# A hybrid decoder layer on one Trainium2 core: the second half's output projection by token tiles, its weights split further ahead, and the FFN operands made in two rounds

## The chip, the core and the metric

The kernel runs on one core of a Trainium2 chip. The core has a matrix engine (TensorE, PE in the profile; PEld is its weight load), a vector engine (VectorE, DVE), a scalar engine (ScalarE, ACT), GpSimd (POOL) and a queue engine for transfers (SyncE, SP). Each engine carries out its own instructions in the order in which they stand; engines wait for each other through semaphores. The metric is the device time in microseconds (us) of one execution; shorter is better. Before the change it is 1290.92 us, the median of three runs (1289.92 to 1294.27).

## What is computed

One decoder layer for a prompt of 1024 tokens and 8 single-token samples, width 1024, everything in float32. What matters here is the middle: a mixer (attention and retention) gives `mix`, an output projection follows, then a layer norm, then a SwiGLU FFN with 2816 hidden columns and a second layer norm.

```python
y = jnp.concatenate([att, ret], -1) @ w_out                       # mixer's end: 1024 x 1024
yp = layer_norm(DEEPNORM_ALPHA * yp + (1.0 + gtp) * mp, ln1_w, ln1_b)
shp, scp, gtp = ada_mod(c_prompt, w_ada_ffn, b_ada_ffn)
g, u = jnp.split((yp * (1.0 + scp) + shp) @ w_up, 2, axis=-1)
fp = (silu(g) * u) @ w_down
yp = layer_norm(DEEPNORM_ALPHA * yp + (1.0 + gtp) * fp, ln2_w, ln2_b)
```

## The kernel before

**Arithmetic.** A float32 product is made of three matmuls of rounded operands (`mm3`, L213 to L217): each operand is split into a high half (a cast by ScalarE) and a low half (a subtraction by VectorE that waits for that cast), and high x high, high x low and low x high are summed in a PSUM bank. There are 8 banks of 128 x 512. All larger tiles in SBUF come from one pool of 46 pages of 128 x 1040 (L186); a new tile waits for the last readers of the page that it takes.

**Order.** `Merge` (L103 to L175) runs one main generator (matmuls) and weaves side generators between its steps by estimated costs; a side generator can wait for a name in the set `done`. A scheduler then fixes each engine's order from the priorities in which this code was run.

**Output projection** (`out_proj`, L1108 to L1166). The tokens are two halves of 512, each of four tiles of 128. A half is done in two column groups of 512 (`cg`), a group in four weight units `kp` of 256 rows. The units of the second half are numbers 54 to 57 (first column group) and 58 to 61 (second); `raw57`, `wh57`, `wl57` are unit 57 as loaded, its high half and its low half. For each unit the four tiles take their products in turn, so all four banks `pout0` to `pout3` of a group are complete only at its end. Sample rows take the unsplit weights in eight small matmuls per group (`poutz`). Then each tile is evacuated: VectorE multiplies the bank by the gate (`otmp`, L1157) and adds the scaled residual (`xr`, L1158).

`depth = [2, 1, 0]` (L285) says how many units ahead of the current one are loaded, get their high half and get their low half (`w_get`, L287). `w_mid` asks for the next unit's low half in the middle of a unit.

**Layer norm 1** (`ln1_tile`, L1202). For each token tile, once both column groups of its half are out (`("out", half)`): statistics on VectorE (L1176, L1181), a power on GpSimd (L1183), normalisation on ScalarE (L1197). `ln1_s` does the same for the sample rows and transposes them (`h2ps`, L1223).

**FFN operands** (`h2_group`, L1235). Group `g` is the half `g`. It needs all four normalised tiles of its half. For each of four blocks `j` it transposes eight 128 x 128 pieces on TensorE (`h2p`), applies the modulation on ScalarE (`ht`, L1253), splits two quarters (`hb`, L1258/L1259), forms four sums and differences (`ts`, L1263 to L1265), splits these (`hs`, L1301/L1302) and splits a last quarter (`hc`, L1271/L1272). A block does all of this before the next one begins.

**FFN up** (`up`, L1489). The product is done by a seven-product scheme with the steps 1, 2, 6, 7, 5, 3, 4 (L1296). Steps 1 and 2 use `hb`, step 3 uses `hc`, the others use `hs`. There are 22 weight matrices. Matrix 0 is first applied to group 0 and then to group 1 (L1583 to L1586); from matrix 1 on both groups are taken together. Each matrix is loaded in two pieces `wr` (L1311), VectorE forms four sums `sb`, `sa` (L1320 to L1323), and four splits `wa`, `wb`, `wc`, `wd` follow. `up_prep` (L1352) sets out these steps by a list of due times; matrix 1 and later wait for the name `ahead`. Matrix 0's load and sums are written down inside `out_proj` at `kp` 2 and 3 of the last column group.

The stages follow each other by these lines (L1764 to L1768): `out_proj(0, False)`; layer norm and operands of half 0 beside `out_proj(1, True)`; layer norm and operands of half 1 beside `ffn()`.

Of the kernel before, what the change touches and what calls it, by code (L numbers as in the profile page):

```python
# [177 lines left out]
def emit(ctx, tc, I, O):  # L178
# [928 lines left out]

    def out_proj(half, with_s):  # L1108
        yield ("need", ("att", half))
        for cg in range(2):  # L1110
            ps = [bank(f"pout{t}") for t in range(4)]
            psz = None
            prev = None
            for kp in range(4):
# [25 lines left out]
                if with_s and kp % 2 == 1:  # L1140
# [4 lines left out]
                    for q in range(4):  # L1145
                        w = (prev if q < 2 else raw)[:, (q % 2) * 512:(q % 2) * 512 + 512]
                        PE.matmul(psz[32 * q:32 * q + 32, :], lhsT=mixTs[:, 4 * (kp // 2) + q, :], rhs=w,
                                  start=kp == 1, stop=kp == 3)
# [4 lines left out]
            cs = slice(cg * 512, (cg + 1) * 512)
            for t in range(4):
                x = xr[half * 4 + t]
                tmp = tmp512("otmp")
                V.tensor_tensor(out=tmp, in0=ps[t], in1=gates[1][:, cs], op=ALU.mult)  # L1157
                V.scalar_tensor_tensor(out=x[:, cs], in0=x[:, cs], scalar=ALPHA, in1=tmp, op0=ALU.mult, op1=ALU.add)  # L1158
            if with_s:
                tmp = tmp512("otmp")  # L1160
                samp_sum(tmp[0:8], psz, 512)
                V.tensor_tensor(out=tmp[0:8], in0=tmp[0:8], in1=gates[1, "s"][0:8, cs], op=ALU.mult)
                x = xrs[0]
                V.scalar_tensor_tensor(out=x[0:8, cs], in0=x[0:8, cs], scalar=ALPHA, in1=tmp[0:8], op0=ALU.mult,
                                       op1=ALU.add)
# [36 lines left out]
    def ln1_tile(t):  # L1202
        yield "need", ("out", t // 4)
# [31 lines left out]
    def h2_group(g):  # L1235
# [8 lines left out]
        for j in range(4):  # L1244
            ht = page(f"ht{g}_{j}")
            hv = ht[:, 0:4 * n].rearrange("p (s b c) -> p s b c", s=2, b=2)
            h3 = ht[:, 0:4 * n].rearrange("p (q c) -> p q c", q=4)
            for s in range(2):
# [12 lines left out]
            HB[g, j] = hb  # L1261
            ts = page(f"ts{g}_{j}")
# [8 lines left out]
            A.copy(out=hc[:, o:o + n], in_=h3[:, 3])  # L1271
            V.tensor_sub(out=hc[:, o + n:o + 2 * n], in0=h3[:, 3], in1=f(hc[:, o:o + n]))  # L1272
# [543 lines left out]
```

## Time and profile before

| what | value |
| --- | --- |
| median of three runs | 1290.92 us |
| the profiled execution, its own time | 1291.37 us |
| its span, first to last instruction | 1289.5 us |
| mean granted TensorE clock | 0.971 |
| before the output projections | 0 to 423.5 us |
| both halves' output projections | 423.5 to 576.3 us |
| first up products until TensorE runs without gaps | 576.3 to 625 us |
| up products (last one starts near 1055 us), then down products (from 1059.8 us) | to the end |

In rows of the timeline the columns are: start in us from the span's start, duration in us, engine, line, operation, tile written <- tiles read, sizes, and how many instructions were merged. A bracket gives the idle time just before the row and what ended it. In a table of windows each engine's busy time in a stretch stands in front of its number of instructions; the last three columns are granted clock (1.00 is full speed), share of the transfer engines, and GB/s.

### The profile page before, as it was taken

The numbers are of one execution on the slowest core, as the hardware profiler recorded it, in microseconds if no ns is written. First come the engines' busy times: TensorE is split into PE (matmuls) and PEld (weight loads), VectorE is DVE, ScalarE is ACT, GpSimd is POOL, SyncE is SP. The second block draws the span as 40 slices with busy tenths as digits, with TensorE's granted clock in tenths as the row PEclk, the third lists the DMA queues.
The fourth block names the chain that finished last, engine by engine and source line by source line (L and its number), as shares of the span: only waits on it lengthen the run. The fifth ranks groups of instructions, "written<-read, shape, count | busy, mean of one in ns | idle before, by whom it ended". The sixth has DMA issues, their size and how long they took to land.

```text
span 1289.5 us, 20190 instructions
## 1 busy us (share of the span) xinstructions
PE 1222.2 (95%) x7922; PEld 1031.0 (80%) x7922; DVE 883.6 (69%) x1712; ACT 449.2 (35%) x812; POOL 159.0 (12%) x170
## 2 busy tenths in 40 slices
PE   8999979899999989696999999999999998999996
PEld 5877756688777667475899999999999986888885
DVE  2456675786654586767676776676676759849697
ACT  2335523344552223516232232323232234524420
POOL 0000032321002242002011110111011110000021
PEclk8999989999999989887999999999999999999998
DMA  9732477152226431602254444444354389846631
GB/s 285 234 110 66 138 250 250 49 176 78 64 67 211 146 101 35 204 1 99 76 178 156 131 138 142 156 148 163 107 179 157 123 313 392 290 158 206 205 129 66
DMA packets 144135, 199.07 MB, mean 154 GB/s; under 512 B 8139, under 2 KB 85171, under 8 KB 144024
## 3 DMA queue, kind: packets, MB, share of 16 engines
q1 hardware_dynamic: 133512, 161.37, 39.1%
q0 software_dynamic: 10528, 36.42, 7.4%
q8 instruction: 62, 1.02, 0.3%
q14 instruction: 33, 0.27, 0.1%
HBM read 155.02 MB, written 43.77 MB: 154 GB/s over the span
## 4 chain that ended last, share of the span: by engine, by line
PE 37%; issue 34%; DVE 8%; POOL 5%; DMA 2%; ACT 1%; POOLq 0%; DVEq 0%; SPq 0%; ACTq 0%
PE dn L216 4%; PE dn L215 4%; PE dn L217 4%; PE pin L215 4%; PE pin L217 3%; PE pin L216 3%; PE pout L216 2%; PE pout L217 2%; PE pout L215 2%; POOL fd L1440 1%; POOL fs L1444 1%; PE adab L874 1%; POOL ws L1473 1%; DVE z L1550 1%; DMA z<-yd 1%
## 5 line engine op out<-in xcount | busy, mean ns | idle before, releaser
L215 PE MATMUL pin<-wh,hT 128*128 128x512 f32 (+1 forms) x320 | 129.3, 408 | 0.1
L216 PE MATMUL pin<-wl,hT 128*128 128x512 f32 (+1 forms) x320 | 125.2, 391 | 3.8 <-DVE wl L281 3.8
L217 PE MATMUL pin<-wh,hT 128*128 128x512 f32 (+1 forms) x320 | 125.2, 392 | 0.4 <-DVE hT L340 0.4
L215 PE MATMUL up<-hb,wa_h 128*128 128x256 f32 (+1 forms) x352 | 100.5, 286 | 0.5 <-ACT tp L1388 0.5
L216 PE MATMUL up<-hb,wa_h 128*128 128x256 f32 (+1 forms) x352 | 100.4, 285 | 0.0
L217 PE MATMUL up<-hb,wa_l 128*128 128x256 f32 (+1 forms) x352 | 100.0, 285 | 0.0
L215 PEld LDWEIGHTS pin<-wh,hT 128*128 128x128 f32 x320 | 61.0, 191 | 26.9 <-issue 13.8
L281 DVE TENSOR_TENSOR wl<-raw,wh 128x1024 fp32r<-128x1024 f32 (+1 forms) x62 | 73.4, 1187 | 7.3 <-ACT wh L269 3.6
L217 PEld LDWEIGHTS pin<-wh,hT 128*128 128x128 f32 x320 | 61.6, 193 | 15.6 <-DVE hT L340 1.7
L216 PEld LDWEIGHTS pin<-wl,hT 128*128 128x128 f32 x320 | 61.8, 193 | 14.5 <-DVE wl L281 4.3
L215 PEld LDWEIGHTS up<-hb,wa_h 128*128 128x128 f32 x352 | 67.3, 191 | 2.1 <-ACT tp L1388 1.0
L1407 ACT ACTIVATE sg<-sg 128x256 f32<-128x256 f32 (+1 forms) x66 | 27.5, 419 | 118.5 <-DVE sg L1406 118.5
L216 PEld LDWEIGHTS up<-hb,wa_h 128*128 128x128 f32 x352 | 67.2, 191 | 0.5 <-DVE hb L1259 0.3
L217 PEld LDWEIGHTS up<-hb,wa_l 128*128 128x128 f32 x352 | 67.2, 191 | 0.1
L216 PE MATMUL pout<-wl,mh 128*128 128x512 f32 x128 | 54.8, 428 | 12.9 <-DVE wl L281 12.9
L269 ACT CAST wh<-raw 128x1024 fp32r<-128x1024 f32 (+1 forms) x62 | 62.6, 1022 | 11.4 <-DMA raw<-in_w_in 6.7
L1183 POOL TENSOR_TENSOR lrs<-lrs,cst 128x1 f32<-128x1 f32 (+1 forms) x18 | 23.7, 1320 | 284.0 <-DVE lrs L1182 218.9
L215 PE MATMUL pout<-wh,mh 128*128 128x512 f32 x128 | 53.2, 424 | 4.2 <-ACT wh L269 4.2
L1412 DVE TENSOR_TENSOR uc<-up,tp 128x256 f32<-128x256 f32 x66 | 28.2, 427 | 39.4 <-PE up L217 39.3
L1406 DVE TENSOR_TENSOR sg<-up,tp 128x256 f32<-128x256 f32 (+1 forms) x66 | 27.8, 423 | 38.4 <-PE up L217 38.4
L1440 POOL DMA_DIRECT2D fd<-sg x33 | 19.8, 600 | 278.7 <-DVE sg L1413 278.7
L217 PE MATMUL pout<-wh,ml 128*128 128x512 f32 x128 | 53.8, 420 | 0.0
(502 smaller groups left out, 3687.8 us busy)
## 6 DMA issues: line engine op xcount, KB each, us to landing
wr<-in_w_up SPq DMA_DIRECT2D x44, 512.0 KB, 5.3
raw<-in_w_in SPq DMA_DIRECT2D x38, 512.0 KB, 3.9
adr<-in_w_ada_ffn SPq DMA_DIRECT2D x24, 512.0 KB, 4.1
wd<-in_w_down SPq DMA_DIRECT2D x22, 512.0 KB, 5.1
dr<-fs SPq DMA_DIRECT2D x44, 256.0 KB, 2.9
dr<-ws SPq DMA_DIRECT2D x44, 256.0 KB, 3.3
fd<-sg POOLq DMA_DIRECT2D x33, 256.0 KB, 3.9
dr<-fd SPq DMA_DIRECT2D x33, 256.0 KB, 7.3
```

Source lines behind the costliest of these rows:

```text
L215: PE.matmul(ps, lhsT=ah, rhs=bh, start=start, stop=False, skip_group_check=onto)
L216: PE.matmul(ps, lhsT=ah, rhs=bl, start=False, stop=False, skip_group_check=onto)
L217: PE.matmul(ps, lhsT=al, rhs=bh, start=False, stop=stop, skip_group_check=onto)
L269: A.copy(out=h[:, 0:n], in_=src[:, 0:n])
L281: V.tensor_sub(out=l[:, 0:n], in0=src[:, 0:n], in1=f(h[:, 0:n]))
L874: PE.matmul(b[32 * q:32 * q + 32, :], lhsT=cT[:, k2 * 4 + q, :], rhs=rr[q // 2][:, (q % 2) * 512:(q % 2) * 512 + 512], start=k2 == 0, stop ...
L1183: G.tensor_tensor(out=rs[0:rows, 0:1], in0=rs[0:rows, 0:1], in1=C("mh")[0:rows, 0:1], op=ALU.pow)
L1406: V.tensor_tensor(out=dst, in0=ps, in1=add, op=ALU.add)
L1407: A.activation(out=dst, in_=dst, func=AF.Silu)
L1412: V.tensor_tensor(out=t, in0=ps, in1=add, op=ALU.add)
L1440: G.dma_start(out=two(d) if p == 4 else d, in_=ap)
L1444: G.dma_start(out=d.rearrange("a p c -> p a c"), in_=t[:, 0:1024].rearrange("p (a c) -> p a c", a=2))
```

## The change

1. While the second half is projected, `depth` is `[3, 2, 1]`: loads, high halves and low halves are asked for one unit earlier.
2. In the second half's second column group, the loop over units takes the products of tile 0 only and keeps the four split units. Then the sample rows are summed, tile 0 is evacuated, and tiles 1, 2 and 3 take all their products one tile after the other, each evacuated when it is done. Each tile has a `done` name of its own (`outt`), so its layer norm can begin. Matrix 0's load is written down after tile 0's evacuation, its sums after tile 1's.
3. `h2_group` makes `ht` and `hb` of all four blocks in a first round and writes the normalised tiles out there; `ts`, `hc` and `hs` of all four blocks follow in a second round. A new name `h2b` stands between the rounds.
4. `ffn` begins matrix 0 on group 1 when `h2b` is there and asks for the second round after three yields; `ahead` is set at `h2b`.
5. Layer norm and operands of half 1 are handed to the weaver before `out_proj(1, True)` is run.

```diff
     def out_proj(half, with_s):
         yield ("need", ("att", half))
+        if half == 1:
+            depth[:] = [3, 2, 1]
         for cg in range(2):
+            by_tile = half == 1 and cg == 1
...
-                if half == 1 and cg == 1 and kp >= 2:
-                    up_prep(-AHEAD[0] if kp == 3 else -AHEAD[1])
...
-                    for t in range(4):
-                        c0 = kk * 512 + t * 128
-                        mm3(ps[t], mh[:, c0:c0 + 128], ml[:, c0:c0 + 128], wh, wl, k == 0, k == 7)
+                    for t in range(1 if by_tile else 4):
+                        unit(kp, kk, t)
                         yield 648
...
+            if by_tile:
+                out_samp(cg, psz)
+                for t in range(4):
+                    if t == 1:
+                        up_prep(-AHEAD[1])
+                    if t == 2:
+                        up_prep(-AHEAD[0])
+                    if t:
+                        for kp in range(4):
+                            for kk in range(2):
+                                unit(kp, kk, t)
+                            yield 1296
+                    out_evac(half, cg, t, ps[t])
+                    done.add(("outt", half * 4 + t))
...
     def ln1_tile(t):
-        yield "need", ("out", t // 4)
+        yield "need", ("outt", t)
...
+        for j in range(4):
+            ht = blocks(j)
...
             HB[g, j] = hb
+            yield 880, 0, 1000
+        for t in range(4 * g, 4 * g + 4):
+            x = xr.pop(t)
+            G.dma_start(out=yd[t], in_=x[:, 0:1024])
+        done.add(("h2b", g))
+        for j in range(4):
+            ht, hts[j] = hts[j], None
...
-        yield ("need", ("h2", 1))
+        yield ("need", ("h2b", 1))
         done.add("ahead")
-        yield from up(0, (1,))
+        for n, r in enumerate(up(0, (1,))):
+            yield r
+            if n == 2:
+                yield ("need", ("h2", 1))
...
         M.add([ln1_tile(t) for t in range(4)] + [h2_group(0)], 2)
+        M.add([ln1_tile(t) for t in range(4, 8)] + [ln1_s(), h2_group(1)], 2)
         M.run(out_proj(1, True), R4)
-        M.add([ln1_tile(t) for t in range(4, 8)] + [ln1_s(), h2_group(1)], 2)
```

Here `unit` is the three matmuls of one tile with one half of a unit, `out_evac` and `out_samp` are the evacuations of a tile and of the sample rows as they were, and `blocks(j)` is the part of a block up to `ht`. The line numbers in the rows below are those of each kernel; the changed kernel's are higher (L1347 is L1302 before, L1112 is L1157, L1113 is L1158, L1212 is L1176).

The first place is VectorE in the first group's operands, where unit 57's low half is made. Before:

```order
L1264 TENSOR_TENSOR ts0_1_4757<-ht0_1_4741,ts0_1_4757 128x256
L1272 TENSOR_TENSOR hc0_0_4724<-ht0_1_4741,hc0_0_4724 128x256
L1265 TENSOR_TENSOR ts0_1_4757<-ht0_1_4741,ts0_1_4757 128x256
L1302 TENSOR_TENSOR hs0_1l_4762<-ts0_1_4757,hs0_1h_4761 128x1024
L1263 TENSOR_TENSOR ts0_2_4801<-ht0_2_4785 128x512
L1259 TENSOR_TENSOR hb0_2_4798<-ht0_2_4785,hb0_2_4798 128x512
L1264 TENSOR_TENSOR ts0_2_4801<-ht0_2_4785,ts0_2_4801 128x256
L1265 TENSOR_TENSOR ts0_2_4801<-ht0_2_4785,ts0_2_4801 128x256
L1302 TENSOR_TENSOR hs0_2l_4806<-ts0_2_4801,hs0_2h_4805 128x1024
L281 TENSOR_TENSOR wl57_4815<-raw57_4680,wh57_4774 128x1024
```

And in the changed kernel, from the first operation of the group on:

```order
L1301 TENSOR_TENSOR hb0_0_4719<-ht0_0_4706,hb0_0_4719 128x512
L1301 TENSOR_TENSOR hb0_1_4738<-ht0_1_4725,hb0_1_4738 128x512
L1301 TENSOR_TENSOR hb0_2_4757<-ht0_2_4744,hb0_2_4757 128x512
L1313 TENSOR_TENSOR ts0_0_4786<-ht0_0_4706 128x512
L1301 TENSOR_TENSOR hb0_3_4776<-ht0_3_4763,hb0_3_4776 128x512
L1314 TENSOR_TENSOR ts0_0_4786<-ht0_0_4706,ts0_0_4786 128x256
L1320 TENSOR_TENSOR hc0_0_4790<-ht0_0_4706,hc0_0_4790 128x256
L1315 TENSOR_TENSOR ts0_0_4786<-ht0_0_4706,ts0_0_4786 128x256
L1320 TENSOR_TENSOR hc0_0_4790<-ht0_1_4725,hc0_0_4790 128x256
L1347 TENSOR_TENSOR hs0_0l_4794<-ts0_0_4786,hs0_0h_4793 128x1024
L281 TENSOR_TENSOR wl57_4806<-raw57_4616,wh57_4686 128x1024
```

Unit 57's low half stood behind three full blocks; now it stands behind the first round and block 0 of the second. Units 58 to 61 stand behind block 3's start and the first column group's evacuation in both kernels.

The second place is VectorE at the end of the second column group, `pout0` to `pout3` being its four tiles. Before, matrix 0's splits come first and then the four tiles together:

```order
L1302 TENSOR_TENSOR wa0_l_5030<-wr0_0_4993,wa0_h_5029 128x1024
L1302 TENSOR_TENSOR wb0_l_5081<-sa0_5023,wb0_h_5080 128x1024
L1157 TENSOR_TENSOR otmp_5061<-pout0_4922,gate1_4049 128x512
L1157 TENSOR_TENSOR otmp_5064<-pout1_4923,gate1_4049 128x512
L1158 SCALAR_TENSOR_TENSOR xr1_0_4855<-xr1_0_4855,otmp_5061 128x512
L1158 SCALAR_TENSOR_TENSOR xr1_1_4857<-xr1_1_4857,otmp_5064 128x512
L1157 TENSOR_TENSOR otmp_5067<-pout2_4924,gate1_4049 128x512
L1157 TENSOR_TENSOR otmp_5070<-pout3_4925,gate1_4049 128x512
```

And in the changed kernel, from tile 0 on:

```order
L1112 TENSOR_TENSOR otmp_4982<-pout0_4926,gate1_4049 128x512
L1119 TENSOR_TENSOR otmp_4975<-otmp_4975,gates_4024 8x512
L1113 SCALAR_TENSOR_TENSOR xr1_0_4853<-xr1_0_4853,otmp_4982 128x512
L1121 SCALAR_TENSOR_TENSOR xrs_4861<-xrs_4861,otmp_4975 8x512
L1212 BN_STATS lst_4995<-xr1_0_4853 128x6
L1112 TENSOR_TENSOR otmp_5023<-pout1_4927,gate1_4049 128x512
L1217 BN_AGGR lmv_4998<-lst_4995 128x2
L1365 TENSOR_TENSOR sb0_5027<-wr0_1_4987 128x512
L1218 TENSOR_SCALAR lrs_4999<-lmv_4998 128x1
L1113 SCALAR_TENSOR_TENSOR xr1_1_4855<-xr1_1_4855,otmp_5023 128x512
L1231 SCALAR_TENSOR_TENSOR lrs_4999<-lmv_4998,lrs_4999 128x1
L1366 TENSOR_TENSOR sa0_5026<-sb0_5027,wr0_0_4985 128x512
```

Tile 0's evacuation and statistics now stand ahead of tile 1's, and matrix 0's sums (`sb0`, `sa0`, which read its load `wr0`) stand between them.

The third place is TensorE where matrix 0 meets group 1 (`up` are banks, `hb1` and `hs1` the group's operands). Before, all that block 0 feeds comes first:

```order
L215 MATMUL up_5376<-hb1_0_5269,wa0_h_5029 128x260
L216 MATMUL up_5376<-hb1_0_5269,wa0_h_5029 128x260
L217 MATMUL up_5376<-hb1_0_5269,wa0_l_5030 128x260
L215 MATMUL up_5403<-hs1_0h_5276,wb0_h_5080 128x260
L215 MATMUL up_5440<-hs1_0h_5276,wc0_h_5115 128x260
```

And in the changed kernel all four blocks of step 1 do:

```order
L215 MATMUL up_5366<-hb1_0_5237,wa0_h_5032 128x260
L216 MATMUL up_5366<-hb1_0_5237,wa0_h_5032 128x260
L217 MATMUL up_5366<-hb1_0_5237,wa0_l_5033 128x260
L215 MATMUL up_5366<-hb1_1_5255,wa0_h_5032 128x260
L216 MATMUL up_5366<-hb1_1_5255,wa0_h_5032 128x260
L217 MATMUL up_5366<-hb1_1_5255,wa0_l_5033 128x260
```

The `hs` products of group 1 moved behind steps 1 and 2 of all blocks. From matrix 2 on the order on every engine is as before.

More of the change, by code (lines that the diff above doesn't have):

```diff
@@ L1106, in emit, with out_evac, out_samp, unit @@
     xrs = []
+    def out_evac(half, cg, t, ps):
+        cs = slice(cg * 512, (cg + 1) * 512)
+        x = xr[half * 4 + t]
+        tmp = tmp512("otmp")
+        V.tensor_tensor(out=tmp, in0=ps, in1=gates[1][:, cs], op=ALU.mult)
+        V.scalar_tensor_tensor(out=x[:, cs], in0=x[:, cs], scalar=ALPHA, in1=tmp, op0=ALU.mult, op1=ALU.add)
+    def out_samp(cg, psz):
+        cs = slice(cg * 512, (cg + 1) * 512)
+        tmp = tmp512("otmp")
+        samp_sum(tmp[0:8], psz, 512)
+        V.tensor_tensor(out=tmp[0:8], in0=tmp[0:8], in1=gates[1, "s"][0:8, cs], op=ALU.mult)
+        x = xrs[0]
+        V.scalar_tensor_tensor(out=x[0:8, cs], in0=x[0:8, cs], scalar=ALPHA, in1=tmp[0:8], op0=ALU.mult, op1=ALU.add)
     def out_proj(half, with_s):
         yield ("need", ("att", half))
+        if half == 1:
+            depth[:] = [3, 2, 1]
         for cg in range(2):
+            by_tile = half == 1 and cg == 1
             ps = [bank(f"pout{t}") for t in range(4)]
             psz = None
-            prev = None
+            raws, ws = [], []
+            def unit(kp, kk, t):
+                h, l = ws[kp]
+                mh, ml = MH[half, kp], ML[half, kp]
+                k, c0 = 2 * kp + kk, kk * 512 + t * 128
+                mm3(ps[t], mh[:, c0:c0 + 128], ml[:, c0:c0 + 128], h[:, kk * 512:(kk + 1) * 512],
+                    l[:, kk * 512:(kk + 1) * 512], k == 0, k == 7)
             for kp in range(4):
@@ L1151, in out_proj @@
+                if not by_tile:
+                    ws[kp] = None
+                    if not with_s:
+                        raws[kp] = None
                 w_free(("out", half, cg, kp))
             yield ("need", "g1")
[L1153 to L1165, printed above, removed]
+            if by_tile:
[12 more added lines that the diff above has]
+                    done.add(("outt", half * 4 + t))
+            else:
+                for t in range(4):
+                    out_evac(half, cg, t, ps[t])
+                if with_s:
+                    out_samp(cg, psz)
+                if cg == 1:
+                    for t in range(4):
+                        done.add(("outt", half * 4 + t))
@@ L1243, in h2_group, with blocks @@
             yield "need", "xns"
-        for j in range(4):
+        def blocks(j):
             ht = page(f"ht{g}_{j}")
             hv = ht[:, 0:4 * n].rearrange("p (s b c) -> p s b c", s=2, b=2)
-            h3 = ht[:, 0:4 * n].rearrange("p (q c) -> p q c", q=4)
             for s in range(2):
```

26 lines of the change are left out of this document (13 added, 13 removed).

## Prediction

> **What bounds the kernel now.** I read the page first, then the stages, then TensorE's own waits from 500 us on, then VectorE and ScalarE over the same stretch.
>
> ```profile
> span 1289.5 us, 20190 instructions
> PE 1222.2 (95%) x7922; PEld 1031.0 (80%) x7922; DVE 883.6 (69%) x1712; ACT 449.2 (35%) x812; POOL 159.0 (12%) x170
> ...
> 423.50:576.30 152.80, 133.92 (x659) 100.84 (x657) 102.66 (x193) 48.46 (x76) 29.06 (x25) 0.93 0.31 102
> 576.30:625.00 48.70, 36.22 (x225) 31.88 (x222) 36.27 (x83) 28.16 (x41) 7.25 (x10) 0.82 0.27 88
> 625.00:930.00 305.00, 303.05 (x2525) 295.53 (x2525) 212.92 (x383) 87.44 (x160) 32.79 (x49) 1.00 0.44 143
> ```
>
> TensorE sets the time: from 625 to 930 it is busy 303.05 of 305.00 us at full clock. It is not so in the two stages that the change touches. After the output projections (576.3 to 625) it is busy 36.22 of 48.70 us at clock 0.82. Whatever TensorE reaches 625 earlier should come off the end, since what follows is dense and in the same order in both kernels.
>
> ```profile
> 535.75 0.80 PE L216 MATMUL pout<-wl,mh 128*128 128x512 f32 x1 [4.86 <-DVE wl L281]
> 536.35 0.63 PE L217 MATMUL pout<-wh,ml 128*128 128x512 f32 x1
> 536.77 0.63 PE L216 MATMUL pout<-wl,mh 128*128 128x512 f32 x1
> ...
> 541.40 0.40 PE L217 MATMUL pout<-wh,ml 128*128 128x512 f32 x1
> 541.63 0.39 PE L215 MATMUL pout<-wh,mh 128*128 128x512 f32 x1
> ...
> 547.42 1.09 PE L215 MATMUL pout<-wh,mh 128*128 128x512 f32 x3 [4.23 <-ACT wh L269]
> 550.22 0.80 PE L216 MATMUL pout<-wl,mh 128*128 128x512 f32 x1 [1.71 <-DVE wl L281]
> ...
> 576.26 0.39 PE L215 MATMUL up<-hb,wa_h 128*128 128x256 f32 x1
> 576.49 0.28 PE L216 MATMUL up<-hb,wa_h 128*128 128x256 f32 x1
> 576.61 0.28 PE L217 MATMUL up<-hb,wa_l 128*128 128x256 f32 x1
> ...
> 592.17 0.66 PE L1223 MATMUL h2ps<-cst,xrs 8*128 8x8 f32 x8 [1.03 <-ACT xrs L1197]
> ...
> 624.13 0.39 PE L217 MATMUL up<-hb,wa_l 128*128 128x256 f32 x1
> ```
>
> TensorE waits 4.86 us for the low half of unit 57, then 4.23 and 1.71 us for unit 58. From start to start a 512-wide matmul takes 0.42 us after such a gap and 0.23 us when warm (536.35 to 536.77; 541.40 to 541.63); a 256-wide one takes 0.12 us warm. The matmul at 624.13 is the first that needs `wa_l` of matrix 1; TensorE runs without a gap behind it, so I measure the change there.
>
> ```profile
> 534.48 1.22 DVE L281 TENSOR_TENSOR wl<-raw,wh 128x1024 fp32r<-128x1024 f32 x1
> ...
> 553.99 2.34 DVE L281 TENSOR_TENSOR wl<-raw,wh 128x1024 fp32r<-128x1024 f32 x2
> 556.26 0.67 DVE L1320 TENSOR_TENSOR sb<-wr 128x512 f32<-128x512 f32 x1
> 556.86 0.67 DVE L1322 TENSOR_TENSOR sa<-wr,wr 128x512 f32<-128x512 f32 x1
> ...
> 573.31 1.38 DVE L1157 TENSOR_TENSOR otmp<-pout,gate 128x512 f32<-128x512 f32 x2 [12.18 <-PE pout L217]
> ...
> 593.45 1.45 ACT L1253 ACTIVATE ht<-h2p,B,A 128x512 f32<-128x512 f32 x2 [0.72 <-PE h2p L1252]
> ...
> 601.33 0.42 DVE L1264 TENSOR_TENSOR ts<-ht,ts 128x260 f32<-128x260 f32 x1
> 601.66 0.42 DVE L1272 TENSOR_TENSOR hc<-ht,hc 128x260 fp32r<-128x260 f32 x1
> 603.55 1.24 DVE L1302 TENSOR_TENSOR hs_1l<-ts,hs_1h 128x1040 fp32r<-128x1040 f32 x1 [1.12 <-ACT hs_1h L1301]
> ...
> 613.74 1.24 DVE L1302 TENSOR_TENSOR hs_3l<-ts,hs_3h 128x1040 fp32r<-128x1040 f32 x1 [1.24 <-ACT hs_3h L1301]
> ```
>
> Behind TensorE's waits stands VectorE. It is full from 518 to 561, then idle 12.18 us until the projection's four banks are complete, and then it has everything left to do while TensorE waits. That idle stretch is the prize.
>
> **The change part by part.** Prices of VectorE, from start to start: 0.60 us for a 512-wide operation (556.26 to 556.86), 0.35 to 0.45 for a 256-wide one, 1.15 for a 1024-wide one, and 1.1 where it must wait for a ScalarE cast (the 1.12 at 603.55).
>
> ```profile
> 503.95 1.39 DVE L1157 TENSOR_TENSOR otmp<-pout,gate 128x512 f32<-128x512 f32 x2 [3.07 <-PE pout L217]
> 514.23 0.38 PE L1252 MATMUL h2p<-cst,xr 128*128 128x128 f32 x2
> 517.04 1.45 ACT L1253 ACTIVATE ht<-h2p,B,A 128x512 f32<-128x512 f32 x2 [0.63 <-PE h2p L1252]
> 518.84 1.06 PE L1147 MATMUL poutz<-raw,mixTs 128*32 128x512 f32 x8
> ...
> 521.95 1.45 ACT L1253 ACTIVATE ht<-h2p,B,A 128x512 f32<-128x512 f32 x2
> 523.43 0.62 ACT L1258 CAST hb<-ht 128x512 fp32r<-128x512 f32 x1
> 523.96 0.40 ACT L1271 CAST hc<-ht 128x256 fp32r<-128x256 f32 x1
> ...
> 592.76 3.71 PE L1252 MATMUL h2p<-cst,xr 128*128 128x128 f32 x32
> ```
>
> *Units split ahead, first group in two rounds.* Unit 56's halves move up to where VectorE waits 3.07 us for TensorE (the row at 503.95), so they cost nothing there; were that wait gone, they would cost 1.15. The first round is ScalarE's: two `ht` and one `hb` per block, 2.0 us (521.95 to 523.96), four blocks from 517.04 to 525.1. Then VectorE needs 0.7 for the last `hb`, 1.1 for block 0's 256-wide sums, 1.1 for the exposed cast and 1.25 for `hs_0l`, and 1.15 for unit 57: done at 530.4, against 535.70 now (534.48 + 1.22). TensorE gets there at 528.3: from 514.2 the order has 40 matmuls (9.3), 32 transposes (3.7, as at 592.76) and 8 sample matmuls (1.1). The 4.86 us wait becomes about 2.
>
> *What is late next.* The second round's rest and the first column group's evacuation stay on VectorE ahead of units 58 to 61. From 530.4 up to unit 58 the order has thirteen 512-wide operations (7.8 us), six of 256 (2.4), three of 1024 (3.5) and one exposed cast (1.1): 545.2. TensorE has 20 matmuls and three sample ones left (5.0), then three that need banks which VectorE empties by 537.4; it is out of work at 537.7 and waits 7.5 us. So one longer wait takes the place of the 4.23 and the 1.71. Another 6.1 us (five, two and two operations) bring unit 59 at 551.4, and 2.9 more (one and two) unit 61 at 554.3, against 556.33 now (553.99 + 2.34): a gain of only 2 us up to here. TensorE's 13 matmuls between units 58 and 59 take 6.0 us with two sample ones even at half clock, so the half clock costs nothing there; each us that it lasts beyond 551.4 costs 0.5.
>
> *The last column group by tile.* From unit 59's low half (551.4) TensorE has 79 matmuls and two groups of sample matmuls left: 79 x 0.232 + 0.3 = 18.6 us, end at 570.1, against 576.26: 6 us. Tiles 0, 1 and 2 end at about 556.4, 559.7 and 564.8, and VectorE's 12.18 us of idle time are filled with their evacuation and statistics and with matrix 0's sums and splits (it did the latter at 556 to 561 until now). By my count it has no gap from 557 on and reaches tile 3 just when TensorE ends it. If the matmuls ended later, VectorE would wait for each us of it.
>
> ```profile
> 580.24 1.28 ACT L1404 ACT_TABLE_LOAD   x1 [0.87 <-PE up L217]
> 588.63 0.56 POOL L1183 TENSOR_TENSOR lrs<-lrs,cst 128x1 f32<-128x1 f32 x1 [1.02 <-DVE lrs L1182]
> 590.89 1.22 ACT L1197 ACTIVATE xrs<-xrs,lrs 8x1024 f32<-8x1024 f32 x1
> ```
>
> After tile 3 remain four 512-wide operations that wait on each other (2.7), `wc_l` between them (1.2), the GpSimd power (0.56) and small ones (0.7): 575.3. ScalarE, held by the table load of 1.28 and a split before, then normalises tile 3 and the sample rows, 1.2 each, to 578.5; 1.3 us more bring the first `ht` (592.17 to 593.45 now): 579.9 against 593.45. The first three tiles' statistics lie beside matmuls by then.
>
> *Second group in two rounds.* This costs time. Now four blocks take 593.45 to 614.98, 21.5 us. In two rounds: 9.1 us to the last `hb`, then four blocks of 3.65, 3.65, 4.85 (with three additions for the gates) and 3.7 us: 24.9 us. `hs_3l` ends at 604.8. From there to `wa_l` of matrix 1: five sums and additions (3.1), 0 to 0.9 by which twelve matmuls outlast them (warm or at half clock), an addition (0.4) and the split (1.2): 4.7 to 5.6. I take 5.6, since today's clock there is 0.82: 610.4. Fourteen matmuls that stood ahead of this point now stand behind it: 1.7 us warm, 3.0 at half clock; I take 2.3, the clock being about to rise. So 612.7 against 624.13: **11.4 us**.
>
> ```profile
> 535.76 94.80 SPq L1311 DMA_DIRECT2D wr<-in_w_up  x8
> ...
> wr<-in_w_up SPq DMA_DIRECT2D x44, 512.0 KB, 5.3
> ```
>
> *The rest.* The number of operations is the same. Matrix 0's load, issued at 535.76 now, is written down only after tile 0's evacuation and takes buffers that units 58 to 61 or the first group's rounds give back. Given back at 546 (unit 58's split) it costs nothing; at 556, after unit 61's, it lands 5.3 us later at 561.3 against a need at 560.5, and costs 0.8. I take 0, being nearer to the many buffers that come free first. The loads of x go behind units 58 and 59 in SP's queue; their data are needed only at 539, and a delay of up to 10 us is hidden.
>
> The profiled execution took 1291.37 us (span 1289.5), 0.45 above the median of 1290.92. 1291.4 - 11.4 = **1280.0 us**. Uncertain are the half clock (1.5 us either way), my rounding of some 130 VectorE operations by 0.02 us (2.5 either way), and waits that the rows of before can't show, which only add (up to 3.5): 1276 to 1286.5 when they don't all fall together.
>
> A rule weighed: the rows show the matmul at half speed from 535.75 to 541.04, 5.3 us after a 4.86 us gap. [...]
>
> **The rivals.**
> 1. *Given back in the second round* (0.13). Two rounds put all four `hb` ahead of all `hs`, and ScalarE and VectorE hand work to each other in the fixed order of their instructions; if each of the second group's eight steps loses 0.7 us more than I count, 5.6 us go: 1285.6. For it: VectorE's waits of 1.1 us per block appear today. Against: those are already in my sum.
> 2. *The half clock holds from 580 into matrix 1* (0.14). In the two rounds TensorE has three to nine matmuls in 2 to 3.6 us. If it stays at half clock, some 33 matmuls on the path cost 0.1 us more, 3.3 us: 1283.3. For it: today's clock of 0.82 in that stretch. Against: most of those matmuls wait for VectorE anyway. [...]
> 3. *Slower: matrix 0's load comes late* (0.05). If its buffers come free only when the column group ends (570), it lands at 575.3; VectorE's first sum, which stands in front of tile 1's addition, waits from 560.5, 14.8 us, and with it all statistics: 1294.8. It decides for slower once the load is issued after 567. For it: the load is written down later than before. Against: it is written down ahead of tile 1's matmuls, so no buffer that these read can be given to it.
> 4. *No net change* (0.06): the filled idle time only moves VectorE's queue, and new waits of 8 to 14 us eat it. Against: VectorE's order shows only one such wait, for tile 0.
>
> **How the numbers follow.** The forecast has 0.62 and is centred on 1280.0; rivals 1 and 2 end at 1285.6 and 1283.3. The range of 1276 to 1286.5 holds these three but for their tails and leaves out rivals 3 and 4. A measurement of this kernel can tell about 0.3%, 3.9 us: faster means below 1287.0. Faster: 0.62 + 0.13 + 0.14 = 0.89; within: 0.06; slower: 0.05.
>
> **What would show it.** Right: TensorE's wait for unit 57 near 2 us; a wait of 7 to 8 us for unit 58; up products beginning near 570; VectorE without a gap over 2 us between 554 and 570; first `ht` of the second group near 580; `wa_l` of matrix 1 near 610. Wrong: VectorE waiting for `wr` near 560 (rival 3), `hs_3l` after 608 (rival 1), or the first `ht` later than 585.

## The result, and the profile after

The changed kernel takes 1280.34 us (median; 1278.84 to 1281.65) against 1291.23 us for the kernel before: ratio 0.9912, 95% interval 0.9891 to 0.9933. The forecast was 1280.0. The profiled execution of the changed kernel took 1281.65 us (span 1279.8), 1.3 above its median. Three executions of the kernels below (1502.75 and 6640.86 us in run 1, 1769.49 us in run 10) were far slower and are in no median here, so that run 1 stands at 1287.4 us and 7.0 us from the changed kernel, not at the 1288.2 and 7.9 from which the expectation of run 5 starts.

First the stages of the changed kernel, the last two cut at the same matmuls as before (columns as there: span, busy time of TensorE, weight loads, VectorE, ScalarE, GpSimd, granted clock, DMA share, GB/s):

```profile
423.50:571.40 147.90, 132.86 (x655) 97.76 (x654) 108.80 (x208) 50.37 (x78) 29.11 (x28) 0.94 0.33 109
571.40:614.40 43.00, 33.96 (x221) 30.34 (x220) 29.94 (x67) 25.39 (x38) 3.89 (x7) 0.88 0.27 87
614.40:920.30 305.90, 303.30 (x2525) 295.69 (x2524) 212.80 (x383) 87.84 (x161) 32.75 (x49) 1.00 0.43 143
```

The dense stage, the same 2525 matmuls, takes 305.9 us (305.0 before). The two stages ahead of it are shorter, by 4.9 and 5.7 us, and VectorE has moved work from the second (36.27 us before, 29.94 now) to the first. TensorE's rows in the timeline of the changed kernel:

```profile
529.58 1.05 PE L1169 MATMUL poutz<-raw,mixTs 128*32 128x512 f32 x2
530.55 0.50 PE L216 MATMUL pout<-wl,mh 128*128 128x512 f32 x1
...
536.38 1.10 PE L215 MATMUL pout<-wh,mh 128*128 128x512 f32 x3
545.06 0.80 PE L216 MATMUL pout<-wl,mh 128*128 128x512 f32 x1 [7.58 <-DVE wl L281]
...
553.12 0.39 PE L215 MATMUL pout<-wh,mh 128*128 128x512 f32 x1
553.44 1.05 PE L1169 MATMUL poutz<-raw,mixTs 128*32 128x512 f32 x4
554.42 0.50 PE L216 MATMUL pout<-wl,mh 128*128 128x512 f32 x1
...
571.41 0.28 PE L215 MATMUL up<-hb,wa_h 128*128 128x256 f32 x1
...
606.16 0.58 PE L216 MATMUL up<-hs_3l,wb_h 128*128 128x260 f32 x1 [0.65 <-DVE hs_3l L1347]
606.54 0.42 PE L217 MATMUL up<-hs_3h,wb_l 128*128 128x260 f32 x1
606.76 0.42 PE L216 MATMUL up<-hs_3l,wc_h 128*128 128x260 f32 x1
...
612.10 0.42 PE L217 MATMUL up<-hb,wa_l 128*128 128x256 f32 x1 [0.36 <-DVE wa_l L1347]
```

Unit 57 is not waited for any more, unit 58 in one wait of 7.58 us. The up products begin at 571.41 (576.26 before), and matrix 1's `wa_l` is first used at 612.10 (624.13 before). VectorE in the same timeline:

```profile
528.71 1.22 DVE L281 TENSOR_TENSOR wl<-raw,wh 128x1024 fp32r<-128x1024 f32 x1
...
551.83 2.34 DVE L281 TENSOR_TENSOR wl<-raw,wh 128x1024 fp32r<-128x1024 f32 x2
555.15 2.12 DVE L408 TENSOR_TENSOR otmp<-otmp,poutz 8x512 f32<-8x512 f32 x3 [0.97 <-ACT otmp L406]
557.96 0.69 DVE L1112 TENSOR_TENSOR otmp<-pout,gate 128x512 f32<-128x512 f32 x1 [0.70 <-PE pout L217]
...
604.86 1.24 DVE L1347 TENSOR_TENSOR hs_3l<-ts,hs_3h 128x1040 fp32r<-128x1040 f32 x1 [1.18 <-ACT hs_3h L1346]
...
610.49 0.43 DVE L1439 TENSOR_TENSOR tp<-up,tp 128x260 f32<-128x260 f32 x1 [1.26 <-PE up L217]
610.83 1.22 DVE L1347 TENSOR_TENSOR wa_l<-wr,wa_h 128x1024 fp32r<-128x1024 f32 x1
```

ScalarE's first `ht` of the second group:

```profile
581.35 1.45 ACT L1288 ACTIVATE ht<-h2p,B,A 128x512 f32<-128x512 f32 x2 [1.34 <-PE h2p L1287]
```

The issue of matrix 0's load on SP's queue:

```profile
535.49 0.99 SPq L1356 DMA_DIRECT2D wr<-in_w_up  x2
```

The 12.18 us in which VectorE stood idle are gone: from 554 to 570 its longest wait is 0.97 us. The first `ht` of the second group comes at 581.35 (593.45 before).

### The profile page after: what moved, and what is told of

Read it like the earlier page. It is cut to its first block, busy times and chain, and to the rows that moved or that the text cites. A ratio compares the mean times of both kernels' runs of the same rounds, so it can differ in the third digit from the quotient of the medians.

```text
span 1279.8 us, 20189 instructions
## 1 busy us (share of the span) xinstructions
PE 1218.8 (95%) x7922; PEld 1026.1 (80%) x7922; DVE 883.8 (69%) x1712; ACT 449.3 (35%) x812; POOL 152.6 (12%) x170
## 4 chain that ended last, share of the span: by engine, by line
PE 36%; issue 34%; DVE 8%; POOL 5%; DMA 2%; ACT 1%; POOLq 0%; DVEq 0%; SPq 0%; ACTq 0%
PE dn L216 4%; PE dn L217 4%; PE dn L215 4%; PE pin L215 4%; PE pin L216 3%; PE pin L217 3%; PE pout L216 2%; POOL fd L1485 1%; PE pout L217 1%; PE pout L215 1%; POOL fs L1489 1%; POOL ws L1518 1%; PE adab L874 1%; DVE z L1595 1%; DMA z<-yd 1%
## 5 line engine op out<-in xcount | busy, mean ns | idle before, releaser
L269 ACT CAST wh<-raw 128x1024 fp32r<-128x1024 f32 (+1 forms) x62 | 62.8, 1022 | 11.4 <-DMA raw<-in_w_in 6.6
L1471 ACT COPY hTs<-sg 128x8 f32<-128x8 f32 x22 | 4.3, 198 | 138.8 <-DVE sg L1458 138.8
```

Source lines behind the costliest of these rows:

```text
L269: A.copy(out=h[:, 0:n], in_=src[:, 0:n])
```

## The experiments

The theory from the prediction: VectorE's work sets the time from 515 to 612, and the change gains because VectorE works where it waited. The rivals: TensorE's waits for units are what counts; or the parts of the change gain each by itself. Twelve kernels, each timed beside the kernel before (ratios are to it, with 95% intervals). Executions come to this stage up to 4.5 us apart, so the last four columns count from the start of the first half's last evacuation: when the up products begin, the first `ht` of the second group, the end of its `hs_3l`, and the start of matrix 1's `wc_l`, all from the timelines.

| kernel | median us | ratio | evacuation | up | ht | hs_3l | wc_l |
|---|---|---|---|---|---|---|---|
| before | 1291.2 | 1 | 503.95 | 72.3 | 89.5 | 111.0 | 123.0 |
| changed | 1280.3 | 0.9912 (0.9891 to 0.9933) | 503.57 | 67.8 | 77.8 | 102.5 | 112.9 |
| 1 no tiles | 1287.4 | 0.9969 (0.9957 to 0.9982) | 503.43 | 66.7 | 84.9 | 109.5 | 119.1 |
| 2 no greater depth | 1287.1 | 0.9962 (0.9950 to 0.9975) | 505.44 | 74.1 | 83.8 | 108.7 | 118.8 |
| 3 one round, group 1 | 1280.3 | 0.9911 (0.9897 to 0.9924) | 501.33 | 67.8 | 77.8 | 101.1 | 111.9 |
| 4 low halves two ahead | 1283.3 | 0.9938 (0.9923 to 0.9953) | 501.43 | 64.6 | 80.1 | 104.9 | 115.1 |
| 5 tiles alone | 1284.5 | 0.9947 (0.9935 to 0.9959) | 503.50 | 72.7 | 82.7 | 105.7 | 116.5 |
| 6 group 1 staggered | 1277.8 | 0.9895 (0.9881 to 0.9909) | 502.70 | 68.0 | 78.0 | 97.7 | 108.5 |
| 7 units in the gap | 1280.7 | 0.9915 (0.9898 to 0.9932) | 501.08 | 54.9 | 75.3 | 101.1 | 111.3 |
| 8 both of these | 1273.5 | 0.9870 (0.9854 to 0.9886) | 500.91 | 54.9 | 75.3 | 93.5 | 105.0 |
| 9 one round, both groups | 1282.4 | 0.9929 (0.9914 to 0.9945) | 502.54 | 68.7 | 78.4 | 103.4 | 115.7 |
| 10 8 and an early load | 1271.1 | 0.9842 (0.9828 to 0.9856) | 501.37 | 54.9 | 75.3 | 93.5 | 102.2 |
| 11 10, both groups staggered | 1264.8 | 0.9796 (0.9778 to 0.9813) | 503.41 | 54.7 | 69.9 | 88.0 | 96.7 |
| 12 11 without tiles | 1265.1 | 0.9802 (0.9789 to 0.9816) | 502.03 | 54.6 | 71.8 | 88.4 | 97.9 |

### Undoing one part at a time

**1, no tiles** (units ahead and rounds stay):

```diff
-            by_tile = half == 1 and cg == 1
+            by_tile = False
...
+                if half == 1 and cg == 1 and kp >= 2:
+                    up_prep(-AHEAD[0] if kp == 3 else -AHEAD[1])
```

> The changed kernel with one part undone: the last column group multiplies all four token tiles together again, as before; units split ahead and the two rounds stay. Theory (the filled idle time of VectorE is the gain): VectorE waits about 12 us again for the projection's end near 571, and then needs the 20.1 us that it needed before (573.31 to 593.45) to the first ht of the second group: 590.6 in place of 581.35, so 9 us slower than the changed kernel, 1289.5 us. Rival (the units ahead and the rounds bring the gain): within 3 us of the changed kernel, 1280 to 1283 us.

Measured 1287.4 us, 7.0 slower than the changed kernel. VectorE's row of this kernel at the projection's end:

```profile
567.13 1.39 DVE L1112 TENSOR_TENSOR otmp<-pout,gate 128x512 f32<-128x512 f32 x2 [8.30 <-PE pout L217]
```

The wait is back, though 8.30 us and not 12; TensorE begins the up products even 1.2 us earlier than in the changed kernel, and yet `ht` is 7.2 us later. That speaks for VectorE: between the evacuation and `ht` it stands idle 6.4 us longer than in the changed kernel.

**2, no greater depth** (tiles and rounds stay):

```diff
-            depth[:] = [3, 2, 1]
+            depth[:] = [2, 1, 0]
```

> The changed kernel with the units split no further ahead than before (depths 2, 1, 0). Theory (VectorE's work, not TensorE's wait, sets the time from 515 to 580): TensorE's 4.9 us wait for unit 57 is back and unit 58 comes at 549 in place of 545, but VectorE does the same work and loses only the 1.15 us of unit 56 that go back behind its gap: 1281.5 us (1280.3 to 1283). Rival (TensorE's waits for units pass on to the end): 4 to 5 us slower, 1284.5 to 1285.5 us.

Measured 1287.1 us, 6.8 slower: the theory's 1281.5 is wrong, and the loss is larger than the rival's. TensorE's waits for units, and then VectorE's:

```profile
535.71 0.56 PE L216 MATMUL pout<-wl,mh 128*128 128x512 f32 x1 [4.11 <-DVE wl L281]
546.45 0.80 PE L215 MATMUL pout<-wh,mh 128*128 128x512 f32 x1 [4.29 <-ACT wh L269]
553.04 0.80 PE L216 MATMUL pout<-wl,mh 128*128 128x512 f32 x1 [2.35 <-DVE wl L281]
```

```profile
561.88 1.40 DVE L408 TENSOR_TENSOR otmp<-otmp,poutz 8x512 f32<-8x512 f32 x2 [4.17 <-ACT otmp L406]
564.93 0.69 DVE L1112 TENSOR_TENSOR otmp<-pout,gate 128x512 f32<-128x512 f32 x1 [1.66 <-PE pout L217]
```

TensorE begins unit 58's low half at 553.04, 6.1 us later after the evacuation than in the changed kernel, with the whole last column group still to do. Now VectorE waits for it, 4.17 us (through ScalarE's copy of the sample rows) and 1.66. In the changed kernel the two engines come to the last column group almost level (VectorE's waits there are 0.97 and 0.70 us); here TensorE is made the later one, and it sets the time.

**3, one round in the second group.** Its block loop is that of the kernel before (`hb`, `ts`, `split`, `hc` of a block, then the next):

```diff
+        if g in (1,):
+            for j in range(4):
+                ht = blocks(j)
...
+                HS[g, j] = split(ts, f"hs{g}_{j}", 4 * n)
...
+            return
```

> The changed kernel with the second group's FFN operands made in one round (block by block, as before); the first group keeps its two rounds. Theory (as the prediction counted: the second group's rounds cost 24.9 us against 21.5): hs_3l ends at 581.4 + 21.5 = 602.9 in place of 606.1; the 9.15 us from there to wa_l of matrix 1 that were seen before replace 6.0 us and 1.7 us of matmuls moved behind: about 1.8 us faster, 1278.5 us. Rival (the rounds let TensorE work while VectorE finishes, and that counts): 2 to 4 us slower, 1282.5 to 1284.5 us.

Measured 1280.3 us, the same as the changed kernel. `hs_3l` is 1.4 us earlier and `wc_l` 1.0: the direction that the expectation counted (1.8 us), smaller, and below what the medians can tell. The second group's two rounds neither gain nor cost anything that these medians show; the rival's 2 to 4 us slower falls.

**4, low halves two units ahead:**

```diff
-            depth[:] = [3, 2, 1]
+            depth[:] = [3, 2, 2]
```

> The changed kernel with low halves split two units ahead (depths 3, 2, 2): unit 57's low half moves ahead of the first group's rounds, unit 58's to where unit 57's stood, so that it is done near 530 in place of 545. Theory (VectorE is the bound): TensorE's wait of 7.6 us for unit 58 all but goes, yet only what VectorE itself saves counts, 1.15 us or two of them: 1278 to 1280 us. Rival 1 (TensorE is the bound there): the whole wait comes off, 1272.7 us. Rival 2 (unit 57's load, issued at 499.8, is not there in time, and VectorE stands before it ahead of the evacuation at 504): 1 to 3 us slower, 1281.5 to 1283.5 us.

Measured 1283.3 us, 3 slower. TensorE's waits there are now 3.21 and 1.32 us in place of 7.58, and the up products begin 3.3 us earlier, but `ht` is 2.3 us later. VectorE in this kernel:

```profile
554.99 1.40 DVE L408 TENSOR_TENSOR otmp<-otmp,poutz 8x512 f32<-8x512 f32 x2 [3.00 <-ACT otmp L406]
557.81 0.69 DVE L1112 TENSOR_TENSOR otmp<-pout,gate 128x512 f32<-128x512 f32 x1 [1.43 <-PE pout L217]
```

It waits 4.4 us for the sample rows and tile 0, where the changed kernel waits 1.7. It comes to this wait just as early as there (50.6 us after the evacuation in both), but TensorE, in its changed order, brings the sample rows 2.0 us later, though it ends the whole projection earlier. So the 2.3 us of `ht` are lost to TensorE's order, not to VectorE's own work, and the theory's 1278 to 1280 is wrong. Rival 2 had the size but not the place: VectorE did not stand before unit 57 ahead of the evacuation (its wait there is 1.42 us, 2.48 in the changed kernel). That the whole wait for unit 58 comes off at the end (rival 1) falls too.

**5, tiles alone** (depths 2, 1, 0, one round in both groups) and **9, tiles and depth** (one round in both groups):

```diff
 # 5 and 9: one round in both groups
+        if g in (0, 1):
...
 # 5 only
-            depth[:] = [3, 2, 1]
+            depth[:] = [2, 1, 0]
```

> The kernel before with the token tiles of the last column group alone: depths 2, 1, 0 and one round in both groups. Theory (TensorE and VectorE are about equally late in the last column group, so that the tiles gain only when the units come earlier too; the rounds are worth nothing by themselves): as the kernel with tiles and rounds but units no further ahead, 1287 us (1286 to 1288.5). Rival 1 (the parts add: 7.9 us for the tiles): 1283.4 us. Rival 2 (the first group's two rounds are what lets the units be split ahead): 1289 to 1291 us.

> The changed kernel with both groups' operands in one round; token tiles and the units' greater depth stay. Theory (units can be split further ahead only where the first group's low halves make room for them, so that depth and the first group's rounds work only together): as the tiles alone, 1284.5 us (1283 to 1286). Rival (the depth does it by itself, the rounds are worth nothing in either group): 1280.3 us.

Measured 1284.5 and 1282.4 us. The tiles alone gain 0.53% (6.8 us): my theory's 1287 is wrong, and rival 1 holds, whose sum is 1284.3 with the 7.0 us of run 1. Depth adds 2 us without the rounds and 6.8 with them; the rounds without depth cost 2.6 (1284.5 to 1287.1) and with it gain 2. Differences of 2 to 3 us are at the edge of what the intervals tell apart, and run 9 lies between its theory (1284.5) and its rival (1280.3). So most of what depth gains it gains together with the rounds; whether either gains anything alone is not shown. The tiles do most of it by themselves. TensorE in run 9 shows why so little comes of depth there:

```profile
545.51 0.80 PE L216 MATMUL pout<-wl,mh 128*128 128x512 f32 x1 [10.58 <-DVE wl L281]
```

### Moving the waits that are left

**6, second group staggered.** One round, but a block's `split` and `hc` are written behind the next block's `ht`, `hb` and `ts`:

```diff
+        prev = None
+        for j in range(4):
+            cur = first(j)                # ht, hb, ts
+            if prev:
+                second(j - 1, *prev)      # split, hc
+            prev = cur
+            yield 880, 0, 3700
...
+        second(3, *prev)
```

> The changed kernel with the second group in one round whose blocks are staggered: ScalarE casts the sums of a block only after it has made the next block's ht and hb, and VectorE takes the low half of a block after the next block's sums. Nothing is left out. Theory (in the second group VectorE and ScalarE wait for each other, 24.75 us of which only 14.6 are VectorE's work): 2.0 us to the first hb, four blocks of 3.65 and 1.5 for the last low half, 18.1 us from the first ht to the end of hs_3l in place of 24.75; TensorE's matmuls, thinner at first, give 1 to 2 us of it back: 4.5 to 6 us faster than the changed kernel, 1275 us. Rival 1 (TensorE is the bound from 580 on, with some 100 matmuls at half clock): 1279 to 1281 us. Rival 2 (one round block by block does no better however it is written, as the run with one round): 1280 us.

Measured 1277.8 us, 2.6 faster than the changed kernel: half of the 4.5 to 6 that the theory gave, and more than either rival. From `ht` to the end of `hs_3l` it takes 19.7 us (24.75 in two rounds, 23.3 block by block in run 3, 18.1 expected), and `wc_l` is 4.4 us earlier. The end of it on VectorE, and its longest wait there:

```profile
595.15 0.42 DVE L1491 TENSOR_TENSOR sg<-up,tp 128x256 f32<-128x256 f32 x1 [1.51 <-PE up L217]
...
599.14 1.24 DVE L1387 TENSOR_TENSOR hs_3l<-ts,hs_3h 128x1040 fp32r<-128x1040 f32 x1 [0.45 <-ACT hs_3h L1386]
```

So the second group did cost hand-overs between VectorE and ScalarE, not VectorE's work: between `ht` and the end of `hs_3l` VectorE is busy 16.3 us in the changed kernel and 15.7 here.

**7, units in the gap:**

```diff
-            depth[:] = [3, 2, 1]
+            depth[:] = [5, 4, 3]
...
-            with tc.high_priority(offset=WPRI[1]):
+            with tc.high_priority(offset=WPRI[1] if j < 57 else 0):
```

> The changed kernel with the units loaded and split still further ahead (depths 5, 4, 3), and the low halves from unit 57 on without their priority, so that those of 57 and 58 go where VectorE waits for the first group's statistics and normalisations (5.0 us from 513.6 in the changed kernel) and not ahead of the evacuation. Theory (VectorE's own work from 519 to 577 is the bound): two low halves of 1.15 us leave that stretch, TensorE's wait for unit 58 goes, and the first ht of the second group comes 2.3 us earlier: 1278 us. Rival 1 (TensorE is the bound): the 7.6 us wait comes off whole, 1273 us. Rival 2 (as in the run with low halves two units ahead, VectorE's waits only move to the sample rows near 555): 1280 to 1283 us.

Measured 1280.7 us; by the medians no change. TensorE's rows:

```profile
556.02 0.28 PE L215 MATMUL up<-hb,wa_h 128*128 128x256 f32 x1
...
562.70 0.58 PE L217 MATMUL up<-hb,wa_l 128*128 128x256 f32 x1 [6.28 <-DVE wa_l L1347]
```

No unit is waited for any more, and the up products begin 12.9 us earlier after the evacuation; but TensorE then waits 6.28 us for VectorE, and `ht` is 2.5 us earlier (2.3 expected), `wc_l` 1.5, which the medians do not show. This is the clearest test: 12.9 us on TensorE are worth 2.5 at `ht` where VectorE is the bound. Rival 1 falls; rival 2 has the time but not the reason, since VectorE has no wait near the sample rows here.

That the 2.3 us came out is in part luck, for the low halves of units 57 and 58 did not go where they were meant to:

```profile
505.99 1.22 DVE L281 TENSOR_TENSOR wl<-raw,wh 128x1024 fp32r<-128x1024 f32 x1
...
510.68 1.23 DVE L281 TENSOR_TENSOR wl<-raw,wh 128x1024 fp32r<-128x1024 f32 x1
```

They stand within the evacuation and the statistics, put off the first group's first `ht` by 2.3 us, and the wait that they were meant to fill stays (5.56 us, 5.01 in the changed kernel). From that `ht` to the second group's it then takes 4.8 us less (59.9 in place of 64.7): the two low halves are gone from there (2.3), and so are VectorE's waits for the sample rows and tile 0 (1.7 in the changed kernel).

**8, both edits.**

> The last two edits together. If both theories hold and they touch different stretches, they add: 2.3 + 5 us faster than the changed kernel, 1273 us. If TensorE is the bound in either stretch, 1276 to 1279 us; if neither holds, 1280 us or more.

Measured 1273.5 us, the sum that was expected if both hold, but not the sum of what the two did alone: in the medians 2.6 us and nothing, together 6.8; at `wc_l` 4.4 and 1.5, together nearly 8. Why they do more together is not shown. VectorE behind the second group's last block:

```profile
593.14 1.24 DVE L1387 TENSOR_TENSOR hs_3l<-ts,hs_3h 128x1040 fp32r<-128x1040 f32 x1 [0.45 <-ACT hs_3h L1386]
594.98 0.43 DVE L1476 TENSOR_TENSOR tp<-up,tp 128x260 f32<-128x260 f32 x1 [0.60 <-PE up L217]
597.22 0.43 DVE L1479 TENSOR_TENSOR tp<-up,tp 128x260 f32<-128x260 f32 x1 [1.81 <-PE up L217]
...
598.36 0.68 DVE L1405 TENSOR_TENSOR sb<-wr 128x512 f32<-128x512 f32 x1
```

Matrix 1's sums need nothing from TensorE and stand behind two operations that wait for it.

**10, early load.** Only matrix 1's load moves, into the second group's first block (`prep_now` takes it off the list of preparations and issues it); the scheduler then places the sums:

```diff
+                if g and j == 0:
+                    prep_now(1, 0)        # matrix 1: up_load
                 prev = cur
```

> The kernel with staggered second group and units in the gap, and matrix 1's load written down with the second group's first block in place of behind its last. Theory (behind hs_3l VectorE waits 0.60 and 1.81 us for TensorE with matrix 1's four sums of 0.6 us queued behind those waits; with the data known to be there earlier the sums are put into the waits): 2 to 2.5 us faster than that kernel, 1271 us. Rival (TensorE, at half clock behind hs_3l, is the bound there): 1273.5 us.

Measured 1271.1 us, 2.4 faster than run 8. The same place in this kernel:

```profile
594.78 0.69 DVE L1407 TENSOR_TENSOR sb<-wr 128x512 f32<-128x512 f32 x1
595.46 0.43 DVE L1484 TENSOR_TENSOR tp<-up,tp 128x260 f32<-128x260 f32 x1
595.81 0.68 DVE L1408 TENSOR_TENSOR sa<-sb,wr 128x512 f32<-128x512 f32 x1
```

Both waits are filled. What VectorE still waits for in the first group (its two rounds), in the same kernel:

```profile
520.90 0.69 DVE L1343 TENSOR_TENSOR hb<-ht,hb 128x512 fp32r<-128x512 f32 x1 [1.31 <-ACT hb L1342]
522.89 0.69 DVE L1343 TENSOR_TENSOR hb<-ht,hb 128x512 fp32r<-128x512 f32 x1 [1.30 <-ACT hb L1342]
524.89 0.69 DVE L1343 TENSOR_TENSOR hb<-ht,hb 128x512 fp32r<-128x512 f32 x1 [0.71 <-ACT hb L1342]
527.71 1.23 DVE L1389 TENSOR_TENSOR hs_0l<-ts,hs_0h 128x1024 fp32r<-128x1024 f32 x1 [0.78 <-ACT hs_0h L1388]
533.65 1.22 DVE L1389 TENSOR_TENSOR hs_1l<-ts,hs_1h 128x1024 fp32r<-128x1024 f32 x1 [0.51 <-ACT hs_1h L1388]
537.94 1.23 DVE L1389 TENSOR_TENSOR hs_2l<-ts,hs_2h 128x1024 fp32r<-128x1024 f32 x1 [1.11 <-ACT hs_2h L1388]
```

**11, both groups staggered:**

```diff
-        if g in (1,):
+        if g in (0, 1):
```

> The same with the first group staggered in one round as well. Theory (VectorE is the bound from 518 to 571, and in the first group's two rounds it still waits 0.71, 0.78, 0.51 and 1.11 us for ScalarE): 2 to 3 us faster than the kernel with the early load, 1268.5 us. Rival (the staggered first group puts unit 59's split and the evacuation further back, and TensorE waits for units again): 1271 us or more.

Measured 1264.8 us, 6.3 faster than run 10, more than twice what the theory gave. I had counted four of the six waits above; all six are 5.7 us, and `ht` is 5.5 us earlier. The changed kernel's and this kernel's VectorE in the same 64 us (columns as in the stages above):

```profile
513.00:577.00 64.00, 56.34 (x266) 39.46 (x264) 49.87 (x87) 29.73 (x38) 6.91 (x12) 0.92 0.32 116
```

```profile
513.00:577.00 64.00, 59.85 (x332) 47.29 (x331) 52.55 (x105) 35.22 (x46) 9.83 (x16) 0.97 0.38 133
```

VectorE is busy 52.55 us in place of 49.87 (40.28 in the kernel before), and one wait of more than 2.1 us is left in it, 4.91 us for the first group's first `ht`. This is the fastest kernel of the study, 2.0% under the kernel before.

**12, the same without tiles:**

```diff
-            by_tile = half == 1 and cg == 1
+            by_tile = False
...
+                if half == 1 and cg == 1 and kp >= 2:
+                    up_prep(-AHEAD[0] if kp == 3 else -AHEAD[1])
```

> The fastest kernel so far (both groups staggered, units in the gap, early load) with the last column group's four token tiles multiplied together again. Theory (the tiles pay by the time that VectorE would otherwise wait for the projection's end): VectorE comes to the evacuation near 552.5, TensorE ends the projection near 557, so VectorE waits some 4.5 us and not 8 to 12; the first ht of the second group comes 4.4 us later: 1269 us. Rival (with TensorE ahead of VectorE everywhere, the order of its tiles no longer matters): 1265 us.

Measured 1265.1 us: the rival. VectorE at the projection's end:

```profile
553.63 1.39 DVE L1112 TENSOR_TENSOR otmp<-pout,gate 128x512 f32<-128x512 f32 x2 [2.37 <-PE pout L217]
```

It waits 2.37 us, `ht` is 1.9 us later and `wc_l` 1.2, which the medians do not show. The tiles were worth 7.0 us in the changed kernel, where VectorE and TensorE came late in turn; with TensorE well ahead nothing that can be measured is left of it.

## Why the prediction was right, point by point

- **Unit 57**: a wait of about 2 us was predicted; there is none. VectorE ended the low half at 529.93 (530.4 predicted), but TensorE came at 530.55 and not at 528.3: the mis-sized term is the 1.1 us for the sample matmuls, of which three groups of 1.06 us stand there (521.64, 528.16 and 529.58). The prediction priced them by their number, but the group of two at 529.58 took 1.05 us, no less than one of four (553.44) or of eight. It cost nothing, since the next wait took it up.
- **Unit 58**: 7.58 us until 545.06 (7.5 until 545.2 predicted); unit 61's low half ended at 554.17 (554.3). The count of VectorE's operations holds within 0.5 us at all three units.
- **Tiles**: the up products begin at 571.41 and not at 570.1. The mis-sized term is again the sample matmuls: 0.3 us for two groups were counted, and the rows from 553.12 to 554.42 show 1.3 with one 0.23 matmul in it, 1.1 for one group; from 547.36 to 549.77, at a granted clock of 0.50, they show 2.41 with one 0.43 matmul in it, 2.0. All nodes behind are late by this: `ht` 581.35 (579.9), `hs_3l` 606.10 (604.8).
- **Second group in two rounds**: 24.75 us from `ht` to `hs_3l` (24.9 predicted). Rival 1 (0.7 us lost at each step) falls.
- **`wa_l` of matrix 1**: 612.10 (610.4). The half clock is in the rows: from 606.54 to 606.76 a matmul takes 0.22 us, not 0.12 (granted clock 0.50 from 605.38 to 612.20), and VectorE waits 1.26 us for those matmuls where at most 0.9 was counted. Rival 2 was right that the clock falls and wrong that it reaches into matrix 1: TensorE waits for `wa_l` in the end, and the fourteen matmuls moved behind it took 1.7 us, at a clock of 1.00 (2.3 counted). 624.13 - 612.10 - 1.7 = 10.3 us, against 11.4 predicted.
- **Matrix 0's load** was issued at 535.49, 0.3 earlier than before; VectorE did not wait for it. Rival 3 falls. Its own sign was set too early: a load issued at 567 would land at 572.3 and give 1291.8 by its sum, which is not yet slower by the 3.9 us that it needs; that begins at 570.
- **Rival 4** falls: no new wait of VectorE is longer than 0.97 us between 554 and 570.
- **The sum**: the two profiled executions differ by 9.7 us, the medians by 10.9, so 11.4 was 0.5 to 1.7 us too much. About 1 us of it is the sample matmuls. Another 0.9 us is lost in the dense stage, which the prediction took as equal: matmul by matmul the changed kernel is 10.55 us ahead at 625 and 9.66 at 930; no run shows why. That the forecast and the median agree to 0.3 us is luck.
- **A reading that was wrong**: the prediction calls VectorE full from 518 to 561 before the change. It is busy 36.1 of 42.6 us there; the rest is mostly the waits of 1.1 us for ScalarE's casts. The sum held, since these waits were in the prices, but the place for a further gain was overlooked.

The sum was right, but two of its reasons were not. The units ahead were counted as a gain of only 2 us up to unit 61; run 2 shows that without them 6.8 are lost, because the projection, then later, makes VectorE wait. And the second group's rounds were counted as a cost of 3.4 us (24.9 against 21.5); run 3 shows 1.4 us of it at `hs_3l`, 1.0 at `wc_l` and none in the medians. What holds is the main reason: the time goes by how long VectorE stands idle. From the evacuation to the second group's first `ht` it is busy 62.9 us before, 60.7 in the changed kernel and 59.3 in run 11, and idle 26.6, 17.1 and 10.6; in the other kernels it is busy 59.4 to 62.0. Run 1 brings the idle time back (23.5) and loses 7.0 us, run 11 takes the waits for ScalarE out of it and gains 6.3, and run 7 shows that TensorE alone is worth little there (12.9 us earlier, `ht` 2.5).

Left open: how the 6.8 us of run 2 divide between later units and the slower matmuls behind TensorE's three waits (512-wide ones start 0.43 us apart from 536.07 to 539.05 and from 553.64 to 556.20, and 0.23 from 556.57 on); no kernel kept TensorE busy in those waits.

## What to carry to other kernels

Before paying for an earlier start on one engine, look what the other does at that moment: here 12.9 us on TensorE brought the next operands 2.5 us forward and left the median where it was, and a reordering worth 7.0 us was worth nothing that could be measured once another wait had gone. Where one engine rounds and another takes the remainder, write the remainder one block later: in the second group that hand-over, and not the work, was 3.6 us against block by block and 5 against two rounds. A load that is written down early lets a scheduler fill waits with what depends on it: 2.4 us in run 10.

## What the runs showed of the hardware

In the kernel before, TensorE's granted clock was 0.50 from 535.75 to 541.04, behind the wait of 4.86 us, and 512-wide matmuls started 0.43 us apart there; from 541.40 to 544.80 it was 1.00, and they started 0.23 us apart. In the changed kernel the clock was 1.00 at the beginning of the wait of 7.58 us and 0.50 before its end (columns as in the stages; TensorE's busy time is the first after the span, the granted clock the third from the end):

```profile
537.12:540.53 3.41, 0.36 (x1) 0.04 (x1) 3.31 (x5) 0.00 (x0) 0.00 (x0) 1.00 1.05 284
540.53:543.94 3.41, 0.00 (x0) 0.00 (x0) 3.34 (x7) 1.52 (x2) 0.00 (x0) 0.50 0.01 3
```

From the end of that wait, at 545.06, to 550.77 it was 0.50, and 1.00 from 551.00 to 591.60.

In run 11 the clock was 0.50 behind a wait of 2.30 us for `wc_l`, which ended at 567.66, and 256-wide matmuls started 0.21 us apart from 568.03 to 570.81 and 0.12 from 571.19 on:

```profile
564.30:567.71 3.41, 1.11 (x10) 0.89 (x9) 3.30 (x8) 2.91 (x3) 1.62 (x3) 1.00 0.13 54
567.71:571.12 3.41, 3.41 (x16) 3.41 (x17) 0.71 (x5) 2.84 (x3) 1.52 (x4) 0.50 0.30 120
```

In the kernel before, a wait of 2.36 us for `wc_l` ended at 583.70, and the clock was 1.00 from 555.00 to 599.20. From 599.30 to 616.40 it was 0.50 there, although TensorE, busy 13.68 of these 17.10 us, had no wait over 1.30 us. What sets the clock these runs do not show.
